# Dilated attention in a decoder layer: the small matmuls of a block gathered into two groups

## The chip, the cores and the metric

The kernel runs on one core of one Trainium2 chip. The metric is the device time of one execution in microseconds (us). The engines are TensorE (PE in the profile, with its weight loads as PEld), VectorE (DVE), ScalarE (ACT), GpSimd (POOL) and SyncE (SP), which issues the DMAs. Each runs its own instructions in the order in which the program gives them, and waits for others through semaphores.

## What is computed

One decoder layer for 1024 tokens of width 1024, in float32: an attention with three groups of dilated windows, then a gated MLP with a short convolution. The change lies in the attention. Cut to that, the reference is:

```python
h = rms_norm(x, mixer_norm)
proj = (h @ w_in).reshape(B, S, 3, 3, 8, 64)          # group, q/k/v, head, width
for g, (window, dilation) in enumerate(((128, 1), (512, 4), (2048, 16))):
    q = rms_norm(proj[:, :, g, 0], q_gain[g]) * 64 ** -0.5
    k = rms_norm(proj[:, :, g, 1], k_gain[g])
    # blocks of 128 queries of one residue class see themselves and the block before
    s = where(mask, q @ k.T, -inf)
    lse = logsumexp(s);  o = exp(s - lse) @ v
weights = softmax(stack(lses))                        # over the three groups
x = x + sum(weights * outs) @ w_out
x = x + (silu(gate) * up) @ w_down                    # MLP, left as it is
```

## The kernel before

**Units and blocks.** The attention is cut into six units: group 2, 1, 0, each in two halves of four heads (`units`, units 0 to 5). A unit has eight blocks of 128 tokens, so there are 48 blocks, numbered 0 to 47. A block in the first place of its residue class sees only itself (`nk` = 1: all blocks of units 0 and 1, every second one of units 2 and 3, and the first of units 4 and 5); the others see the block before too (`has_prev`, `nk` = 2).

**Large and small matmuls of a block.** `project(k)`, k = 0 to 7, makes q and k of the block in the PSUM tile `qk`: three matmuls of 512 columns for each k (lines 207 to 209), because every operand is kept as a rounded high part and a low part. `project_v(k)` does the same for v in the tile `vp` with three of 256 columns (lines 216 to 218). These two are the main stream of TensorE. The tile `qk` has two PSUM buffers and `vp` has one (`bufs=1`).

Between them stand the small matmuls: `heads_T` (tile `tr`, four transposes of q and k), `scores` (tile `s`, 6 matmuls for nk = 1, or 12 on half the rows for nk = 2), `weights_T` twice (tile `pt`, 2 or 4 transposes of the softmax weights each time), `attend` twice (tile `u`, 4 or 8 matmuls each). Below, tr4, s6, pt2, u8 and so on mean so many matmuls of that tile in a row.

**Work on the other engines.** For each block, in this order: `norm` (ACT squares `qk`, line 223; DVE sums it, line 225; POOL takes the root), `values` (ACT copies `vp` to `v`, line 236; DVE subtracts to get the low part, line 237; after that `vp` is free for the next block), `scale` (DVE, line 229), `heads_split` (ACT and DVE empty `tr` into qT and kT), `softmax` (four times a DVE operation on `s` and an exponential on ACT, lines 320 and 323), `weights_split` twice (ACT and DVE empty `pt` into `pT`, lines 337 and 338), `finish` (DVE reduces `u`, line 356; in units 4 and 5 `merge` follows with one more DVE operation, line 398).

**What sets the order.** Every step is put into a list with a time (`at(...)`), the list is sorted by time, and each engine gets its instructions in that order. One unit of that time is one k of `project`, and a block takes eight. For block i the steps start from e = 8 i + 8, and the table `T` holds each step's offset, so `w0=8.3` puts the first `weights_T` at e + 8.3. A `project_v(k)` stands at 8 i + 0.85 k + 2.6. The offset `bd` is added to `scores` and `softmax` of blocks without a block before. These times only order the instructions; on the chip each starts when its operands and buffers are ready.

**PSUM.** Eight banks: `qk` 2, `vp` 1, `u` 1, tag `tr` 2 (for `tr` and `pt`), tag `s` 2 (for the two halves of the scores; in unit 0 also `xT`, the transposes of the normed input).

**After the attention.** From N = 384 on that time axis, `out_project` (tile `y`) with its weight tiles `wo` takes the place of the main stream, while the last two blocks of attention are still being finished.

Of the kernel before, what the change touches and what calls it, by code (L numbers as in the profile page):

```python
# [8 lines left out]
F32 = mybir.dt.float32  # L9
# [8 lines left out]
P = 128  # L18
# [13 lines left out]
LA = 2  # L32


T = dict(v=2.6, vs=0.85, w=3.1, norm=-0.2, val=0.6, kept=3.2, scale=2.5, hT=4.2, hs=4.45, sc=6.45,
         sm=6.5, w0=8.3, ws0=9.35, w1=10.0, ws1=11.95, mw=10.0, a0=12.2, a1=13.3, mo=12.2,
         fin=14.4, t0=4, so0=3.2, so1=3.3, so2=5.1, so3=5.2, to0=-3.43, to=-3.6, n2=3.0, n2s=5.8,
         xf=-9.8, xs=-5.0, xt=-3.5, wp=1, bd=0.5, bh=0)


@with_exitstack
def trunk(ctx: ExitStack, tc: tile.TileContext, x, mixer_norm, ffn_norm, w_in, q_gain, k_gain,
# [47 lines left out]
    pa = tc.tile_pool(name="pa", bufs=1, side="right", reuse_waits="tile")  # L90
# [4 lines left out]
    PA = ppa.__enter__()  # L95
# [96 lines left out]
    class Block:  # L192
# [67 lines left out]
                        nc.gpsimd.tensor_copy(kT[hd, z, :, :P], self.prev.own(z, e))  # L260

        def heads_T(self):
            self.tr = PA.tile([P, 4, P], F32, name="tr", tag="tr", bufs=2)
            for j in range(4):
                nc.tensor.transpose(self.tr[:, j], self.qn[:, 2 * j:2 * j + 2], ident)  # L265

# [58 lines left out]

        def weights_T(self, p):
            lo, nk = self.lo, self.nk
            self.pt[p] = pt = PA.tile([P, 2, nk, P], F32, name="pt", tag="tr", bufs=2)
            for e in range(2):
                for j in range(nk):  # L330
                    nc.tensor.transpose(pt[:, e, j], self.sm[:, 2 * p + e, lo + j * P:lo + (j + 1) * P],
                                        ident)
# [74 lines left out]
    def at(t, f, *args):  # L407
        plan.append((t, len(plan), f, args))

    xs = {}  # L410
# [48 lines left out]
    for i in range(8):  # L459
        t = early[i] if i < 2 else (8 * i - 12, 8 * i + T["xf"], 8 * i + T["xs"], 8 * i + T["xt"])  # L460
        at(t[0], get_x, i)
# [19 lines left out]
    for u in range(6):  # L481
        wt = {}
        for kt in range(KT):
# [3 lines left out]
            elif kt < SP:  # L487
                t = 64 * u - 32 + T["wp"] + 4 * kt
                lead = t - 3
            else:  # L490
                t = 64 * u - KT + (3.9, *((8.7, 9.45, 10.6, 12.6) if u % 2 == 0 else (5.4, 8.7, 9.6, 10.8)))[kt - SP]
                lead = max(t - 8, 64 * u - KT + (kt - SP - 3) * 1. + T["w"] + .5) if kt < SP + 3 else wt[kt - 3] + .3
            wt[kt] = t
            at(lead, load_raw, u, kt)
            at(t, load_w, u, kt)
    for i, b in enumerate(blocks):
        b.prev = blocks[i - 1] if b.has_prev else None
        for k in range(KT):
            at(8 * i + k, b.project, k)
            at(8 * i + T["vs"] * k + T["v"], b.project_v, k)  # L500
        e = 8 * i + 8
        for name, (step, *args) in dict(
                norm=(b.norm,), val=(b.values,), kept=(b.kept,), scale=(b.scale,), hT=(b.heads_T,),
                hs=(b.heads_split,), sc=(b.scores,), sm=(b.softmax,), w0=(b.weights_T, 0),
                ws0=(b.weights_split, 0), w1=(b.weights_T, 1), ws1=(b.weights_split, 1),
                mw=(b.merge_weights,), a0=(b.attend, 0), a1=(b.attend, 1), mo=(b.merge_others,),
                fin=(b.finish,)).items():
            late = not b.has_prev and (T["bd"] if name in ("sc", "sm") else T["bh"] if name in ("hT", "hs") else 0)
            if b is blocks[-1] and name in ("norm", "val"):
                late = 1.5 if name == "norm" else .3  # L510
            at(e + T[name] + late, step, *args)


    N = 8 * len(blocks)
# [6 lines left out]
    class M:  # L521

        wo, ol, oT, x1, n2, h, pt = {}, {}, {}, {}, {}, {}, {}
# [301 lines left out]
            at(t + 14.6 + .5 * (i == 5), odd, i, 1, nc.gpsimd)  # L825
            at(t + 14.7 + .5 * (i == 5), odd, i, 2, nc.vector)
    t = N + T["t0"] + 42
    at(N + 15, lambda: pa.__exit__(None, None, None))
    at(N + 15.1, make_bt)
    at(t - 20, conv_consts, 0)  # L830
    at(t - 12, conv_consts, 1)
    at(t - 12, pairs[0].load)
# [164 lines left out]
    for n in range(3, NF + 1):  # L997
        old, p, new = pairs[n - 1], *((pairs + [None] * 3)[n:n + 2])
# [7 lines left out]
        if p is None:  # L1006
            for m in range(8):
                b, i = divmod(m, 4)
                pool, tag, bufs = (M.PL, "b", 2) if m < 2 else (M.PR, "ac"[m % 2], 3)
# [97 lines left out]
```

## Time and profile before

| | |
|---|---|
| median of 3 runs | 1303.2 us (1301.95 to 1303.62) |
| the profiled execution: its time, its span | 1301.99 us, 1300.0 us |
| TensorE busy, of the span | 1274.2 us (98%) |
| VectorE, ScalarE, GpSimd busy | 896.2, 617.1, 486.7 us |
| attention without its start and end, 25 to 578 us | TensorE busy 548.79 of 553.00 us |
| end of the attention, 578 to 612 us | TensorE busy 30.55 of 34.00 us |
| the rest, to the end | TensorE busy 678.90 of 688.00 us |

The time is that of the whole execution; the span is from the first instruction to the last in the profile. TensorE's matmuls overlap, and the ends that the profile gives them are modelled, so the starts of successive matmuls tell more than their durations: in the main stream a matmul of 512 columns starts some 0.23 us after the one before, and one of 256 columns some 0.12 us. "Idle before" in a row counts only gaps over 0.15 us.

### The profile page before, as it was taken

The page shows a single profiled execution, that of the slowest core. Times are in us where ns is not written, and L with a number is a line of the kernel's source. Part 1 is how long each engine was busy: PE and PEld are TensorE (multiplying, and loading weights), DVE is VectorE, ACT ScalarE, POOL GpSimd, SP SyncE. Part 2 cuts the span into 40 slices and gives each one's busy share as a digit, 9 for nine tenths or more (in the row PEclk, how much of TensorE's full clock was granted, in tenths as well). Part 3 has the DMA queues.
Part 4 walks back from the last instruction along what each step waited for, and adds up shares of the span by engine and source line. Part 5 has one row for each costly group of instructions (what it writes and reads, how often), then busy time and mean ns, then how long its engine had stood idle before and what let it go on. Part 6 is the DMA issues. An engine that isn't in the chain of part 4 may idle for free.

```text
span 1300.0 us, 19219 instructions
## 1 busy us (share of the span) xinstructions
PE 1274.2 (98%) x6911; PEld 1071.0 (82%) x6911; DVE 896.2 (69%) x1542; ACT 617.1 (47%) x1284; POOL 486.7 (37%) x596
## 2 busy tenths in 40 slices
PE   7999999999999999999998999999999999999998
PEld 6888888888888888887886788888888887888887
DVE  5665555555555665557876988888888888876664
ACT  5555454444464454345644454544544545444441
POOL 4333443332454555535523544444444442000000
PEclk9999999999999999999999999999999999999999
DMA  7112112111131221023711333233233229963341
GB/s 263 38 54 79 38 38 60 47 48 52 46 109 51 62 63 37 27 70 132 235 35 43 120 122 122 81 114 105 66 122 122 81 81 326 367 212 97 97 143 63
DMA packets 111614, 132.16 MB, mean 102 GB/s; under 512 B 6126, under 2 KB 80030, under 8 KB 111518
## 3 DMA queue, kind: packets, MB, share of 16 engines
q1 hardware_dynamic: 111518, 130.93, 31.5%
q8 instruction: 55, 0.90, 0.3%
q14 instruction: 41, 0.34, 0.1%
HBM read 95.91 MB, written 35.00 MB: 101 GB/s over the span
## 4 chain that ended last, share of the span: by engine, by line
PE 43%; DVE 4%; ACT 2%; issue 1%; DMA 1%; POOL 0%; SPq 0%; DVEq 0%; POOLq 0%; ACTq 0%
PE y L902 15%; PE ua L718 15%; PE uc L718 8%; PE ub L718 4%; DVE c L763 2%; ACT c L761 1%; DMA x<-in_x 1%; DMA graw<-gde 0%; DVE bt L629 0%; DVE sz L691 0%; DVE c L774 0%; DVE xn L595 0%; DMA wB<-in_ffn_w_down 0%; DVE sy L687 0%; POOL b L629 0%
## 5 line engine op out<-in xcount | busy, mean ns | idle before, releaser
L902 PE MATMUL y<-wd,g 128*128 128x512 f32 x924 | 210.4, 389 | 0.2
L902 PEld LDWEIGHTS y<-wd,g 128*128 128x128 f32 x924 | 173.4, 188 | 36.9 <-DVE wd L629 0.6
L207 PE MATMUL qk<-w,hh 128*128 128x512 f32 x384 | 157.5, 410 | 0.1
L208 PE MATMUL qk<-w,hh 128*128 128x512 f32 x384 | 152.8, 398 | 0.3 <-DVE w L189 0.3
L209 PE MATMUL qk<-w,hl 128*128 128x512 f32 x320 | 126.1, 394 | 0.0
L79 POOL TENSOR_SCALAR ms<-ss 128x8 f32<-128x8 f32 (+1 forms) x64 | 12.8, 201 | 296.6 <-DVE ss L225 254.0
L763 DVE SCALAR_TENSOR_TENSOR c<-uu,cw,c 128x1023 f32<-128x1023 f32 (+1 forms) x44 | 97.0, 2205 | 37.1 <-ACT c L761 36.3
L216 PE MATMUL vp<-w,hh 128*128 128x256 f32 x384 | 122.0, 318 | 0.4 <-DVE v L237 0.2
L217 PE MATMUL vp<-w,hh 128*128 128x256 f32 x384 | 107.9, 281 | 0.0
L549 POOL TENSOR_TENSOR wyl<-sy,wyh 128x1024 fp32r<-128x1024 f32 x21 | 56.9, 2708 | 109.3 <-issue 55.3
L80 POOL TENSOR_TENSOR rs<-ms,half 128x8 f32<-128x8 f32 (+1 forms) x64 | 89.0, 1391 | 5.3
L218 PE MATMUL vp<-w,hl 128*128 128x256 f32 x320 | 90.0, 281 | 0.0
L323 ACT ACTIVATE sm<-sm,ust 128x128 f32<-128x128 f32 (+1 forms) x128 | 53.3, 418 | 77.0 <-DVE ust L320 74.5
L216 PEld LDWEIGHTS vp<-w,hh 128*128 128x128 f32 x384 | 72.8, 189 | 15.2 <-DVE v L237 2.4
L225 DVE TENSOR_REDUCE ss<-qn 128x8 f32<-128x512 f32 x48 | 32.9, 685 | 75.6 <-ACT qn L223 75.6
L276 ACT ACTIVATE qT<-tr,gains 128x256 fp32r<-128x256 f32 x48 | 22.7, 474 | 122.0 <-PE tr L265 122.0
L217 PEld LDWEIGHTS vp<-w,hh 128*128 128x128 f32 x384 | 72.8, 190 | 9.1
L279 DVE SCALAR_TENSOR_TENSOR qT<-tr,gains,qT 128x256 fp32r<-128x256 f32 x48 | 23.1, 482 | 81.4 <-ACT kT L278 81.4
L208 PEld LDWEIGHTS qk<-w,hh 128*128 128x128 f32 x384 | 73.1, 190 | 1.5 <-DVE w L189 1.0
L207 PEld LDWEIGHTS qk<-w,hh 128*128 128x128 f32 x384 | 73.0, 190 | 0.7 <-ACT hh L116 0.5
L320 DVE CUSTOM_DVE_ANT_0 sm<-s,mask 128x128 f32<-128x128 f32 (+1 forms) x192 | 56.0, 347 | 24.0 <-PE s L298 18.5
L209 PEld LDWEIGHTS qk<-w,hl 128*128 128x128 f32 x320 | 60.5, 189 | 14.6 <-DVE hl L117 0.2
(193 smaller groups left out, 3395.7 us busy)
## 6 DMA issues: line engine op xcount, KB each, us to landing
uraw<-in_ffn_w_up SPq DMA_DIRECT2D x44, 512.0 KB
raw<-in_attn_w_in SPq DMA_DIRECT2D x48, 384.0 KB
wB<-in_ffn_w_down SPq DMA_DIRECT2D x44, 256.0 KB
graw<-gds SPq DMA_DIRECT2D x44, 256.0 KB
gdo<-c SPq DMA_DIRECT2D x11, 512.0 KB
gds<-gbc SPq DMA_DIRECT2D x11, 512.0 KB
graw<-gdo SPq DMA_DIRECT2D x22, 256.0 KB
ud<-ust SPq DMA_DIRECT2D x32, 132.0 KB
```

What stands on the lines that cost most here:

```text
L80: nc.gpsimd.tensor_tensor(r[:, :n], t[:, :n], half[:, :n], op=ALU.pow)
L207: nc.tensor.matmul(self.qk, a, w[:, 0, :512], start=k == 0, stop=False)
L208: nc.tensor.matmul(self.qk, a, w[:, 1, :512], start=False, stop=False)
L209: nc.tensor.matmul(self.qk, b, w[:, 0, :512], start=False, stop=k == KT - 1)
L216: nc.tensor.matmul(self.vp, a, w[:, 0, 512:], start=k == 0, stop=False)
L217: nc.tensor.matmul(self.vp, a, w[:, 1, 512:], start=False, stop=False)
L218: nc.tensor.matmul(self.vp, b, w[:, 0, 512:], start=False, stop=k == KT - 1)
L320: nc.vector.tensor_tensor_reduce(out=sm[:, h, lo:], in0=src[h], in1=m, op0=ALU.add, op1=ALU.min, scale=-1.0, scalar=3e38, accum_out=st[:, ...
L549: eng.tensor_sub(l, raw, h.bitcast(F32))
L718: nc.tensor.matmul(acc[:, lo:hi], w[z][:, s + k], a[y][:, j, k, lo:hi], start=begin and lo == 0 and k == 0 and n == 0, stop=k == 3 and n == 2,
L763: nc.vector.scalar_tensor_tensor(c[:, k:], u[:, :S - k], cw[:, 2 - k, j:j + 1], c[:, k:], op0=ALU.mult, op1=ALU.add)
L902: nc.tensor.matmul(y, gs[:, z, ts], ws[:, w], start=f and n == 0, stop=k == NK - 1 and n == 2, skip_group_check=True)
```

## The change

In each block the small matmuls now stand in two groups. The first has both `weights_T` of a block and `heads_T` of the next block; the second has `scores` of that next block and both `attend` of the block. To that end the table `T` is changed, and PSUM is shared out otherwise: `heads_T` takes a buffer of the tag `s` in all units but the first, and for nk = 1 the two `weights_T` write two halves of one tile. Closing the pool of the attention's tiles moves from N + 15 to N + 17.2, since `finish` is later.

```diff
-T = dict(v=2.6, vs=0.85, w=3.1, norm=-0.2, val=0.6, kept=3.2, scale=2.5, hT=4.2, hs=4.45, sc=6.45,
-         sm=6.5, w0=8.3, ws0=9.35, w1=10.0, ws1=11.95, mw=10.0, a0=12.2, a1=13.3, mo=12.2,
-         fin=14.4, ...
-         xf=-9.8, xs=-5.0, xt=-3.5, wp=1, bd=0.5, bh=0)
+T = dict(v=2.6, vs=0.85, w=3.1, norm=-0.2, val=0.6, kept=3.2, scale=2.5, hT=4.2, hs=4.45, sc=7.01,
+         sm=7.06, w0=12.1, ws0=12.5, w1=12.15, ws1=12.55, mw=10.0, a0=15.02, a1=15.03, mo=12.2,
+         fin=16.1, ...
+         xf=-9.8, xs=-5.0, xt=-3.5, wp=1, bd=0, bh=0)
...
-            self.tr = PA.tile([P, 4, P], F32, name="tr", tag="tr", bufs=2)
+            self.tr = PA.tile([P, 4, P], F32, name="tr", tag="s" if self.u else "tr", bufs=2)
...
-            self.pt[p] = pt = PA.tile([P, 2, nk, P], F32, name="pt", tag="tr", bufs=2)
+            if nk == 2:
+                self.pt[p] = PA.tile([P, 2, nk, P], F32, name="pt", tag="tr", bufs=2)
+            else:
+                if p == 0:
+                    self.pt4 = PA.tile([P, 4, 1, P], F32, name="pt", tag="tr", bufs=2)
+                self.pt[p] = self.pt4[:, 2 * p:2 * p + 2]
+            pt = self.pt[p]
...
-    at(N + 15, lambda: pa.__exit__(None, None, None))
-    at(N + 15.1, make_bt)
+    at(N + 17.2, lambda: pa.__exit__(None, None, None))
+    at(N + 17.3, make_bt)
```

TensorE, a block without a block before, before the change: the row ahead of the scores, the scores (tile `s`, two halves), and what follows up to the first transposes of the weights.

```order
L218 MATMUL vp<-w,hl 128x256
L294 MATMUL s_1865<-kT,qT 128x256 x3
L294 MATMUL s_1866<-kT,qT 128x256 x3
L207 MATMUL qk<-w,hh 128x512
L208 MATMUL qk<-w,hh 128x512
L209 MATMUL qk<-w,hl 128x512
L216 MATMUL vp<-w,hh 128x256
L217 MATMUL vp<-w,hh 128x256
L218 MATMUL vp<-w,hl 128x256
L207 MATMUL qk<-w,hh 128x512
L208 MATMUL qk<-w,hh 128x512
L209 MATMUL qk<-w,hl 128x512
```

The same place with the change, from the last `project` of the block to the first `project_v` behind the group.

```order
L209 MATMUL qk<-w,hl 128x512
L295 MATMUL s_1846<-kT,qT 128x256 x3
L295 MATMUL s_1847<-kT,qT 128x256 x3
L356 MATMUL u<-v,pT 128x128
L358 MATMUL u<-v,pT 128x64
L356 MATMUL u<-v,pT 128x128
L358 MATMUL u<-v,pT 128x64
L356 MATMUL u<-v,pT 128x128
L358 MATMUL u<-v,pT 128x64
L356 MATMUL u<-v,pT 128x128
L358 MATMUL u<-v,pT 128x64
L216 MATMUL vp<-w,hh 128x256
```

The scores stood ahead of the last `project` of the next block and now stand behind it, with both `attend` right behind them. From the scores to the first `project_v` (k = 0) of the block after, TensorE had s6 qk vp qk pt2 vp qk pt2 qk; it now has s6 u8 vp qk vp qk qk. For nk = 2 it had s12 vp qk vp qk pt4 vp qk pt4 qk, and now has s12, u8 or u16 (by the block whose weights are attended), vp qk vp qk qk.

VectorE, unit 5, before the change, from the sum of squares of a block on (`ss`: `norm`; `v`: `values`; `mt<-u` and `o`: `finish` and `merge`):

```order
L225 TENSOR_REDUCE ss_6795<-qn 128x8
L237 TENSOR_TENSOR v<-vp,v 128x4x64
L338 TENSOR_TENSOR pT<-pt,pT 128x512
L370 TENSOR_REDUCE nm<-mt 128x4
L372 TENSOR_TENSOR e<-nm,mt 128x12
L229 TENSOR_TENSOR qn<-qk,rs 128x512
L338 TENSOR_TENSOR pT<-pt,pT 128x512
L386 RECIPROCAL rz<-z 128x4
L279 SCALAR_TENSOR_TENSOR qT<-tr,gains,qT 128x256
L282 SCALAR_TENSOR_TENSOR kT<-tr,gains,kT 128x2x128
L356 TENSOR_REDUCE mt<-u 128x256
L398 TENSOR_TENSOR o<-mt,f 128x256
```

VectorE at the same place with the change (line 363 is the old line 356, 405 the old 398):

```order
L225 TENSOR_REDUCE ss_6764<-qn 128x8
L363 TENSOR_REDUCE mt<-u 128x256
L405 TENSOR_TENSOR o<-mt,f 128x256
L237 TENSOR_TENSOR v<-vp,v 128x4x64
L377 TENSOR_REDUCE nm<-mt 128x4
L379 TENSOR_TENSOR e<-nm,mt 128x12
L229 TENSOR_TENSOR qn<-qk,rs 128x512
L393 RECIPROCAL rz<-z 128x4
L280 SCALAR_TENSOR_TENSOR qT<-tr,gains,qT 128x256
L283 SCALAR_TENSOR_TENSOR kT<-tr,gains,kT 128x2x128
```

The reduction of `u`, and in units 4 and 5 the merge behind it, stood ahead of the softmax and now stand between the sum of squares and the low part of `v`; both subtractions of `pT` have moved behind qT and kT.

## Rows read from the trace of the kernel before

**Rows 1.** The page's first line.

```profile
span 1300.0 us, 19219 instructions
```

**Rows 2.** Stretches: us, PE, PEld, DVE, ACT, POOL busy (count), clock, DMA.

```profile
25.00:578.00 553.00, 548.79 (x3670) 482.67 (x3671) 318.72 (x887) 268.54 (x778) 240.06 (x447) 1.00 0.18 54
578.00:612.00 34.00, 30.55 (x182) 24.33 (x179) 23.82 (x53) 18.69 (x45) 17.18 (x27) 1.00 0.39 134
```

**Rows 3.** TensorE's waits, 25 to 578: who waited for whom, us, times, longest.

```profile
PE tr L265 <- DVE qn L229: 2.9, 5, 0.9
PE pt L331 <- ACT sm L323: 0.3, 1, 0.3
...
PE vp L216 <- DVE v L237: 0.2, 1, 0.2
```

**Rows 4.** Timeline of TensorE, unit 4: start, duration, engine, line, tile, count.

```profile
408.19 0.38 PE L331 MATMUL pt<-ident,sm 128*128 128x128 f32 x2
408.33 0.48 PE L207 MATMUL qk<-w,hh 128*128 128x512 f32 x1
408.64 0.39 PE L208 MATMUL qk<-w,hh 128*128 128x512 f32 x1
...
409.11 0.28 PE L216 MATMUL vp<-w,hh 128*128 128x256 f32 x1
...
409.45 0.40 PE L207 MATMUL qk<-w,hh 128*128 128x512 f32 x1
...
410.16 0.27 PE L216 MATMUL vp<-w,hh 128*128 128x256 f32 x1
...
413.46 0.22 PE L349 MATMUL u<-v,pT 128*128 128x128 f32 x1
...
413.82 0.36 PE L216 MATMUL vp<-w,hh 128*128 128x256 f32 x1
414.02 0.28 PE L217 MATMUL vp<-w,hh 128*128 128x256 f32 x1
```

**Rows 5.** Timeline of DVE there, block 33, behind scores of nk = 1.

```profile
407.66 0.69 DVE L225 TENSOR_REDUCE ss<-qn 128x8 f32<-128x512 f32 x1 [1.71 <-ACT qn L223]
408.26 0.41 DVE L237 TENSOR_TENSOR v<-vp,v 128x256 fp32r<-128x256 f32 x1
```

**Rows 6.** Timeline of DVE and PE, block 34, behind scores of nk = 2.

```profile
419.73 0.41 DVE L237 TENSOR_TENSOR v<-vp,v 128x256 fp32r<-128x256 f32 x1
...
420.79 0.28 PE L216 MATMUL vp<-w,hh 128*128 128x256 f32 x1
```

**Rows 7.** Timeline of DVE: `finish` and `merge` of a block in unit 4.

```profile
414.02 0.69 DVE L356 TENSOR_REDUCE mt<-u 128x256 f32<-128x512 f32 x1
414.82 0.46 DVE L398 TENSOR_TENSOR o<-mt,f 128x256 f32<-128x256 f32 x1
```

**Rows 8.** Timeline of DVE and PE where `vp` was late, block 7.

```profile
105.69 0.42 DVE L237 TENSOR_TENSOR v<-vp,v 128x256 fp32r<-128x256 f32 x1
...
106.16 0.38 PE L216 MATMUL vp<-w,hh 128*128 128x256 f32 x1
106.38 0.28 PE L217 MATMUL vp<-w,hh 128*128 128x256 f32 x1
```

**Rows 9.** Timeline of PE and DVE in unit 0, with `xT`.

```profile
63.07 1.04 PE L114 MATMUL xT<-ident,xn 128*128 128x128 f32 x8
...
65.66 1.29 DVE L117 TENSOR_TENSOR hl<-xT,hh 128x512 fp32r<-128x512 f32 x2
...
66.85 0.87 PE L294 MATMUL s<-kT,qT 128*128 128x256 f32 x6
```

More of the change, by code (lines that the diff above doesn't have):

```diff
@@ L32 @@
 LA = 2
-T = dict(v=2.6, vs=0.85, w=3.1, norm=-0.2, val=0.6, kept=3.2, scale=2.5, hT=4.2, hs=4.45, sc=6.45,
-         sm=6.5, w0=8.3, ws0=9.35, w1=10.0, ws1=11.95, mw=10.0, a0=12.2, a1=13.3, mo=12.2,
-         fin=14.4, t0=4, so0=3.2, so1=3.3, so2=5.1, so3=5.2, to0=-3.43, to=-3.6, n2=3.0, n2s=5.8,
-         xf=-9.8, xs=-5.0, xt=-3.5, wp=1, bd=0.5, bh=0)
+T = dict(v=2.6, vs=0.85, w=3.1, norm=-0.2, val=0.6, kept=3.2, scale=2.5, hT=4.2, hs=4.45, sc=7.01,
+         sm=7.06, w0=12.1, ws0=12.5, w1=12.15, ws1=12.55, mw=10.0, a0=15.02, a1=15.03, mo=12.2,
+         fin=16.1, t0=4, so0=3.2, so1=3.3, so2=5.1, so3=5.2, to0=-3.43, to=-3.6, n2=3.0, n2s=5.8,
+         xf=-9.8, xs=-5.0, xt=-3.5, wp=1, bd=0, bh=0)
 @with_exitstack
```

## Prediction

> **What bounds the kernel now.** [...] Then the waits: the transposes of the heads wait for VectorE's scaling of q and k, 2.9 us in five places; everything else over 0.15 us is small, with one wait of `vp` for VectorE's low part of `v` (0.2 us) [rows 3]. That last row matters most here, because `vp` has one buffer: the first `project_v` of a block cannot start before VectorE has done line 237 of the block before. In most blocks this wait is absent, but the room is small. Behind scores of nk = 1, VectorE ends `v` at 408.26 + 0.41 = 408.67 [rows 5] and TensorE starts `vp` at 409.11 [rows 4]: a slack of 0.44 us. Behind scores of nk = 2 it is 420.79 - 420.14 = 0.65 us [rows 6]. The work of the change is to move things on both sides of this slack, so I follow it through.
>
> **What a small matmul costs.** Two transposes start at 408.19, and the main stream goes on at 408.33; its next matmul follows 0.31 us later instead of 0.23 (408.33 to 408.64) [rows 4]. So the two cost 0.14 + 0.08 = 0.22 us, 0.11 each. Four matmuls of `attend` cost 413.82 - 413.46 = 0.36, and 0.08 for the late second matmul behind them (413.82 to 414.02, against 0.12), together 0.44 us, 0.11 each [rows 4]. A group costs its number of matmuls times 0.11 us, whether it has two or four, and I find no fixed price for a group. The change neither adds nor removes a matmul, so gathering them gives TensorE nothing by itself: I take 0, with a bound that the rival below prices. One step of `project_v` takes 409.45 - 409.11 = 0.34 us and one of `project` 410.16 - 409.45 = 0.71 us [rows 4].
>
> **The slack of `vp`, step by step.** The chain on the other side is: scores, four exponentials of the softmax, the square of `qk`, the sum of squares, (now also `finish`), the low part of `v`. It starts with the scores, so I count from there. The order of TensorE between the scores and the next `vp` loses one `project` (0.71), and both `weights_T`, and gains both `attend`; with nk = 2 it loses one `project_v` (0.34) besides. VectorE's chain gains the reduction of `u`. A reduction of the same 0.69 us lets the next operation start 0.60 us later (407.66 to 408.26) [rows 5], so I take 0.60. In units 4 and 5 it also gains the merge: the start moves from 414.02 to 414.82, and then 0.46 less the overlap of 0.09 [rows 5, 7], so 0.80 + 0.37 = 1.17 in all.
>
> Scores of 6, attend of 8 (16 blocks of units 0 to 2): 0.44 - 0.71 - 0.44 + 0.88 - 0.60 = -0.43 us.
> Scores of 12, attend of 8 (8 blocks): 0.65 - 0.34 - 0.71 - 0.88 + 0.88 - 0.60 = -1.00 us.
> Scores of 12, attend of 16, with the merge (10 blocks of units 4 and 5): 0.65 - 0.34 - 0.71 - 0.88 + 1.76 - 1.17 = -0.69 us.
> Scores of 12, attend of 8, with the merge (2 blocks): -1.00 - 0.57 = -1.57 us.
> Scores of 6, attend of 16: 0.44 - 0.71 - 0.44 + 1.76 - 0.60 = +0.45 us, no wait (8 blocks); with the merge -0.12 (1 block).
>
> A negative slack is a wait of TensorE, and a wait costs a little more than its lateness. Block 7 shows it: `v` ends at 106.11, `vp` starts at 106.16, and its second matmul comes 0.22 us later (106.38) instead of 0.12, since its weights were not loaded ahead [rows 8]. So 0.05 + 0.10 = 0.15 us are added each time. That gives 16 x 0.58 = 9.3, 8 x 1.15 = 9.2, 10 x 0.84 = 8.4, 2 x 1.72 = 3.4 and 0.3: **30.6 us of new waits**. Nothing covers them, since all that is queued behind the waiting `vp` on TensorE is the main stream, and the chain starts anew from each block's scores, so a wait in one block doesn't buy slack in the next.
>
> **Other new waits.** In unit 0, `xT` and the scores share two buffers. VectorE ends the second low part of `xT` at 65.66 + 1.29 = 66.95, and the scores need that buffer for their second half at 66.85 + 3 x 0.12 = 67.21 [rows 9]: a slack of 0.26. With the change both subtractions of `pT` stand ahead of that low part. They are as long as line 237 (0.41, less the overlap of 0.09, so about 0.32 each [rows 5]); TensorE comes 0.71 - 0.44 = 0.27 later. Slack 0.26 - 0.64 + 0.27 = -0.11, so 0.26 us in each of six blocks: 1.6 us. In the other units `tr` and `s` share the tag `s`, but the scores wait for the emptying of `tr` anyway, as qT and kT. The transposes of the weights and the `attend` now come microseconds after their softmax and their split, and should wait for nothing.
>
> **What goes.** TensorE reaches `heads_T` later in its row than VectorE reaches `scale`, which also lost a subtraction of `pT` ahead of it. So I let the five waits of `tr` go: 2.9 + 5 x 0.10 = 3.4 us (bounds 0 and, with every idle time of the stretch, 4.2 [rows 2, 3]). At the end of the attention, 34.00 - 30.55 = 3.45 us are idle [rows 2], in part because scores, softmax, weights and `attend` of the last blocks follow each other closely with no main stream between. They now stand further apart. I take 2.0 us (bounds 0 and 3.45), since the split of the output weights, which TensorE also waits for there, is not moved. That `finish` of the last block is later costs nothing as far as I see: the tiles that reuse its memory are written after two more `out_project`, some 12 x 0.23 us each.
>
> **The sum.** 30.6 + 1.6 - 3.4 - 2.0 = +26.8 us on the profiled execution's 1302.0 us: 1328.8 us. That execution is 1.2 us below the median of the runs, within their spread.
>
> **Rivals.**
> *Only the blocks with 12 scores wait.* If the start of `finish` or of the square overlaps more than I count, the 16 blocks at -0.43 lose most of their wait, and the others some 0.4 us each. The sum is then 8 x 0.75 + 10 x 0.44 + 2 x 1.3 = 13 us, less 5.4: 1310 us. For it speaks that -0.43 is a difference of five numbers; against it, that the durations repeat from block to block.
> *Faster: the chain to `v` is never last.* Should VectorE's `v` be ready in time in all blocks (it would have to come 0.58 us earlier in most and 1.15 us in eight), only what goes is left: 1302.0 - 5.4 = 1296.6 us. The order of VectorE, with the reduction of `u` ahead of `v`, speaks against it.
> *A group has a fixed price.* If the 0.08 us by which the main stream is late behind a group were paid once per group and not for the last weight load, 239 groups becoming 98 would give 141 x 0.08 = 11.3 us. With the waits of `vp` that is 1317.5 us; without them, 1285. Against it: 0.22 for two and 0.44 for four leave no room for a constant [rows 4]. [...]
> [...]
>
> **How the numbers follow.** Chances: the forecast 0.80, with its own range from 1316 (the wait costs its lateness alone, the 16 blocks wait 0.3 us, the end gives 3.45) to 1338 (the waits of `tr` stay, the end gives nothing, and blocks at the change of units, with weight splits on VectorE, wait a microsecond more); only blocks with 12 scores 0.09; never last 0.06; fixed price 0.03; clock 0.02. The range from 1308 to 1338 holds the first two. Within 0.2% (2.6 us, about what a measurement of this kernel can tell from no change) lies only a mixture of these, 0.03. Faster has 0.07, slower 0.90.
>
> **What would show it.** Right: a wait of `vp` line 216 for DVE line 237 at the top of TensorE's waits, some 36 times, 0.4 to 1.6 us each, longest where 12 scores stand before 8 of `attend`; no wait in the blocks with 6 scores and 16 of `attend`; the row of `tr` gone; VectorE's timeline with the reduction of `u` between line 225 and line 237. Wrong: `vp` starting 0.2 us or more after VectorE's `v` has ended, a granted clock under 1.00 in the attention, or matmuls of a group spaced closer than 0.11 us.

## The result and the profile after

The changed kernel takes 1342.5 us (median of four runs, 1341.6 to 1343.0) against 1302.6 for the kernel before: 1.031 times as long, with a 95% interval from 1.0295 to 1.032. The profiled execution has a span of 1340.9 us, 40.9 more than [rows 1]. The direction of the forecast (1329, slower) was right, its size was not: 40 us were lost where 26.8 were counted, and the time lies above the range.

All of the loss lies before the MLP. In the timelines of TensorE the last `qk` starts at 616.36 instead of 579.34 (+37.0), the last `y` of the output projection at 687.54 instead of 646.67 (+40.9), and the end comes 40.9 later too. The first line of the page after, and the first rows of TensorE's waits (who waited for whom, us in total, times, longest; line 237 is still the low part of `v`, 266 is `heads_T`, 188 and 189 are the high and low part of the weights, 117 the low part of `xT`):

```profile
span 1340.9 us, 19130 instructions
```

```profile
PE vp L216 <- DVE v L237: 25.2, 34, 2.7
...
PE s L295 <- DVE hl L117: 3.5, 5, 0.7
PE qk L207 <- ACT w L188: 2.2, 2, 1.7
...
PE tr L266 <- DVE qn L229: 1.3, 2, 0.9
...
PE qk L208 <- DVE w L189: 1.0, 2, 0.5
```

The row of `vp` was one wait of 0.2 us in [rows 3]; it is now the first of all. The row of `tr` fell from five waits to two, of which one stands in the attention and one behind it. New are `s` behind `xT`, and `qk` behind weights. The stretch of the attention (columns as in [rows 2]) shows that TensorE is still the engine with the most work, but idle for 31.7 of 575 us instead of 4.2 of 553, and that the clock was not quite full:

```profile
25.00:600.00 575.00, 543.28 (x3544) 471.12 (x3543) 308.04 (x861) 261.43 (x760) 230.72 (x433) 0.99 0.16 50
```

A regular block of unit 4 (scores of 12, `attend` of 16, with the merge), DVE and then PE (start, duration, engine, line, operation, tile):

```profile
461.04 0.69 DVE L225 TENSOR_REDUCE ss<-qn 128x8 f32<-128x512 f32 x1 [1.66 <-ACT qn L223]
461.64 0.68 DVE L363 TENSOR_REDUCE mt<-u 128x256 f32<-128x512 f32 x1
462.43 0.42 DVE L405 TENSOR_TENSOR o<-mt,f 128x256 f32<-128x256 f32 x1
462.77 0.42 DVE L237 TENSOR_TENSOR v<-vp,v 128x256 fp32r<-128x256 f32 x1
...
463.24 0.39 PE L216 MATMUL vp<-w,hh 128*128 128x256 f32 x1 [0.59 <-DVE v L237]
463.46 0.28 PE L217 MATMUL vp<-w,hh 128*128 128x256 f32 x1
```

In [rows 5] line 237 followed line 225 directly. Now `finish` and the merge stand between, 1.13 us from start to start (461.64 to 462.77). `v` ends at 463.19, `vp` starts 0.05 later, and its second matmul comes 0.22 later instead of 0.12: the wait costs what [rows 8] said. The weight loads of these two matmuls (PEld), first at [rows 8] in the kernel before, then here, and for comparison in the kernel before where `vp` doesn't wait [rows 4]:

```profile
106.16 0.19 PEld L216 LDWEIGHTS vp<-w,hh 128*128 128x128 f32 x1 [0.58 <-DVE v L237]
106.27 0.19 PEld L217 LDWEIGHTS vp<-w,hh 128*128 128x128 f32 x1
```

```profile
463.24 0.19 PEld L216 LDWEIGHTS vp<-w,hh 128*128 128x128 f32 x1 [1.02 <-DVE v L237]
463.35 0.19 PEld L217 LDWEIGHTS vp<-w,hh 128*128 128x128 f32 x1
```

```profile
408.88 0.19 PEld L216 LDWEIGHTS vp<-w,hh 128*128 128x128 f32 x1
409.11 0.19 PEld L217 LDWEIGHTS vp<-w,hh 128*128 128x128 f32 x1
```

Without a wait the first load starts 0.23 us ahead of its matmul and the second with the first matmul (409.11); behind the wait the first starts with its matmul (463.24) and the second 0.11 later, 0.11 ahead of its own.

**Where the 40.9 us are.** To add waits up I take, for each pair of neighbouring TensorE instructions, the time from start to start over the usual one of the same kind. The table has all such delays over 0.14 us, by what released them (us, attention alone unless said). The late second matmul behind a wait of `vp` is 0.10 and has a row of its own. The end is taken from the first `qk` of the last block to the last `y`, so that it holds the same matmuls before and after; the wait of `vp` in it (0.8) stands in the rows above and is taken out here.

| | before | after | change | counted in the prediction |
|---|---|---|---|---|
| `vp` for `v`, its first matmul | 0.9 | 30.6 (34 waits) | +29.7 | +30.6, with the next row |
| the late second matmul behind it | 0.3 | 3.6 | +3.3 | in the row above |
| scores for `xT`'s low part, unit 0 | 0 | 4.3 (5) | +4.3 | +1.6 |
| `qk` for weights, at unit boundaries | 0.6 | 4.1 (4) | +3.4 | 0 |
| `tr` for `qn` | 3.8 | 0.6 (1) | -3.2 | -3.4 |
| `pt` for the softmax | 0.7 | 0 | -0.7 | 0 |
| the end, first `qk` of the last block to last `y` | 79.3 | 80.3 | +1.0 | -2.0 |
| two stretches at half clock | 0 | about 3.4 | +3.4 | 0 |
| sum | | | +41.2 | +26.8 |

The sum is 0.3 more than the 40.9 measured; the rest lies at the start and in differences below 0.14. So the large term was 2.4 us short, and four others were missing, too small or had the wrong sign. The rest of this text is about both.

### The profile page after: what moved, and what is told of

Its sections match the earlier page's. It is cut to its first block, busy times and chain, and to the rows that moved or that the text cites. A ratio compares the mean times of both kernels' runs of the same rounds, so it can differ in the third digit from the quotient of the medians.

```text
span 1340.9 us, 19130 instructions
## 1 busy us (share of the span) xinstructions
PE 1286.7 (96%) x6911; PEld 1073.9 (80%) x6911; DVE 895.4 (67%) x1542; ACT 616.7 (46%) x1284; POOL 484.0 (36%) x596
## 3 DMA queue, kind: packets, MB, share of 16 engines
q1 hardware_dynamic: 111518, 130.93, 30.6%
## 4 chain that ended last, share of the span: by engine, by line
PE 43%; DVE 4%; ACT 1%; issue 1%; POOL 1%; DMA 0%; SPq 0%; DVEq 0%; POOLq 0%; ACTq 0%
PE ua L725 16%; PE y L909 15%; PE uc L725 8%; PE ub L725 4%; DVE c L770 1%; ACT c L768 0%; DVE bt L636 0%; DMA wB<-in_ffn_w_down 0%; DVE xn L602 0%; POOL b L636 0%; DVE sz L698 0%; DVE x L595 0%; POOL wzl L556 0%; POOL wxl L556 0%; DVE c L781 0%
## 5 line engine op out<-in xcount | busy, mean ns | idle before, releaser
L216 PE MATMUL vp<-w,hh 128*128 128x256 f32 x384 | 119.4, 311 | 25.2 <-DVE v L237 25.2
```

What stands on the lines that cost most here:

```text
L216: nc.tensor.matmul(self.vp, a, w[:, 0, 512:], start=k == 0, stop=False)
```

## Experiments

Each is a change to one of the kernels; the numbers are medians, with the kernel before (1302.1 to 1302.8) run beside them on the same chip.

**1. Finish behind `v`.** One number of the table:

```diff
-         fin=16.1,
+         fin=16.7,
```

> The changed kernel, with one number of the table other: fin 16.7 instead of 16.1, so that a block's finish (and merge) stands behind the next values on VectorE and no longer ahead of them. Chain theory (scores, softmax, Square, its sum, finish, v, then vp): each wait of vp falls by the 0.60 us of the finish, by 1.17 where merge goes with it. From the waits of the changed kernel: 16 blocks 0.41 to 0, 8 blocks 1.05 to 0.45, 10 blocks 0.73 to 0, 2 blocks 1.60 to 0.43, the four long ones at unit boundaries by 0.6 each: -6.6 -4.8 -7.3 -2.3 -2.4 = -23, so about 1319 us, vp's waits about 4 us in sum instead of 25.2. Rival: what holds v is the copy of vp on ScalarE or the exponentials, not the finish: no change, 1342. Second rival: the finish now delays the scale of the heads, and waits of tr take the place of half of the gain: 1330.

Measured: 1326.5 us, 15.9 less than the changed kernel (1.0182 of before, 1.0167 to 1.0197).

```profile
PE vp L216 <- DVE v L237: 8.0, 15, 2.2
...
PE tr L266 <- DVE qn L229: 2.7, 4, 0.9
```

So `finish` ahead of `v` is on the path. From start to start the waits of `vp` fell from 30.6 to 10.4, and the late second matmuls behind them from 3.6 to 1.6, together by 22.2 us. Against this, 1.7 came back as waits of `tr` (the second rival, but far smaller than it said), 0.6 as waits of `qk` for low parts, the second stretch at half clock was twice as long (about 1.7; the mean granted clock of the profiled run is 0.995, in the changed kernel 0.997), and the end, taken as in the table, is 1.2 longer, with more waits for output weights. The four longest waits fell by 0.5 to 0.6 each, about as expected. What was too large in the 23 is its first term: of the 16 waits of 0.41 the changed kernel has eight.

**2. Scores apart again.** Scores and softmax go back ahead of the last projection; all else stays:

```diff
-sc=7.01,
-         sm=7.06,
+sc=6.45,
+         sm=6.5,
...
-bd=0,
+bd=0.5,
```

> The changed kernel with scores and softmax back ahead of the last projection (sc 6.45, sm 6.5, bd 0.5), so that scores and attend no longer stand together; the transposes of weights and heads stay one group, attend and finish stay late. Chain theory: scores end a projection of 0.69 us earlier (0.69 and a step of vp, 1.02, in blocks with a previous one), and the waits of vp fall by that: 0.41 to 0, 1.05 to 0.03, 0.73 to 0, 1.60 to 0.58: -6.6 -8.2 -7.3 -2.0, the four long ones -2.8, and the clock's two falls behind waits go, -3: -30, so about 1312. Rival, that a group has a price of its own: 48 more groups at 0.08 to 0.1 give 4 to 5 us back, 1317. Rival, that the waits come from the finish's place alone: the finish stays where it is, 1342.

Measured: 1326.4 us (1.0182, 1.0166 to 1.0197), half of what was expected.

```profile
PE vp L216 <- DVE v L237: 6.5, 6, 2.4
PE s L295 <- DVE hl L117: 6.3, 5, 1.3
```

In units 2 to 5 most regular blocks wait no more for `vp`, as the chain says (in unit 5 a block takes 12.60 us instead of 13.43): there a projection more between scores and `vp` is enough. Of the six waits that the row has left, four stand where the changed kernel had its longest ones. But the scores, 0.7 us earlier, wait longer for `xT` in unit 0, and come too early for the split of the heads elsewhere: in a block of unit 1 the six scores take 0.93 us to the next instruction's start instead of 0.71, `vp` is still 0.22 late instead of 0.42, and the block takes 11.4 us as without this edit. The clock, too, is still at half for 6.8 us in all, where I had expected no fall. So the place where the change put the scores has a reason of its own, and 1312 was out of reach by this edit.

**3. Room for a second `vp`.** The wait's cause is taken away: `vp` shares three buffers with the weights' transposes, in the order of instructions of the changed kernel.

```diff
-                self.vp = PA.tile([P, 256], F32, name="vp", bufs=1)
+                self.vp = PA.tile([P, 512], F32, name="vp", tag="tr", bufs=3)[:, :256]
...
-        tag, bufs = ("vp", 1) if i else ("s", 2)
+        tag, bufs = ("tr", 3) if i else ("s", 2)
```

> The changed kernel in its order of instructions, but vp shares three buffers with the weights' transposes instead of having one of its own, so that a block's first product of values need not wait for the copy of the block before. Chain theory: all waits of vp go (25.2 us), and with the two long ones the falls of the clock (3 to 4 us); nothing else is late in a block, since the next user of the chain is attend, seven projections later: about 1314 us. Rival, that the wait only moves to the next that needs VectorE (tr, whose scale stands behind v, or s, behind the softmax): half of it comes back, 1328. Waits of s in unit 0 (3.5 us), of qk at the boundaries and the tail stay in either case.

Measured: 1314.4 us (1.0093, 1.0078 to 1.0109), the number of the chain theory.

```profile
PE qk L207 <- ACT w L188: 4.1, 4, 1.8
PE tr L266 <- DVE qn L229: 3.3, 5, 1.0
PE s L295 <- DVE hl L117: 3.0, 5, 0.7
PE qk L208 <- DVE w L189: 2.0, 4, 0.5
```

No wait of `vp` is left; 28.1 us of the 40 are gone, and one of the two stretches at half clock with them (the mean granted clock is 0.999 instead of 0.997). But the number was met by luck. From start to start 34.2 us of `vp` and about 1.7 of the clock went, and 6.4 came back: `qk` is now late for weights by 7.8 us instead of 4.1, and `tr` by 3.3 instead of 0.6. So the waits did move in part, as the rival said, by a fifth instead of half; the expectation missed this, and missed as much on the other side, since it took the 25.2 us of idle time in the row of `vp` and not the delay from start to start (30.6) with the second matmuls (3.6).

The run also settles whether gathering pays: the distance from one block's first `qk` to the next one's, in undisturbed blocks, is 10.89 us in unit 1 and 12.60 in unit 5 with this order, 10.85 and 12.57 in the kernel before. Two groups in a block instead of five save nothing.

**4. The buffers alone.** The kernel before in its own order, with the change's two edits of buffers: `tr` under the tag `s` (unit 0 apart), and one tile `pt4` for both halves of a block's turned weights.

```diff
-            self.tr = PA.tile([P, 4, P], F32, name="tr", tag="tr", bufs=2)
+            self.tr = PA.tile([P, 4, P], F32, name="tr", tag="s" if self.u else "tr", bufs=2)
...
+                if p == 0:
+                    self.pt4 = PA.tile([P, 4, 1, P], F32, name="pt", tag="tr", bufs=2)
+                self.pt[p] = self.pt4[:, 2 * p:2 * p + 2]
```

> The kernel before in its own order, with the change's buffers alone: heads' transposes in the scores' buffers, both weight transposes of a block without a previous one in one tile. If the order alone costs, this is as fast as before or gains what the five waits of tr hold, 2.9 us: 1299.7 to 1302.6. If the buffers cost too (the scores wait for the heads' copies, or the second transposes for the first copy out of the shared tile), waits of s or pt appear and it is slower, by 0.2 to 0.4 in each of 40 blocks: 1310 to 1318.

Measured: 1347.5 us (1.034, 1.0323 to 1.0357), more than the changed kernel itself.

```profile
PE pt L337 <- DVE pT L344: 34.0, 26, 3.4
```

The second half of the weights is turned only after the first half has been copied out, since both lie in one tile; I had allowed 0.4 us for it, and it is up to 3.4. In the changed kernel both halves are turned before either is copied, so this price isn't paid there. It shows that buffers and order of this change belong together. What `tr` under the tag `s` costs alone was not tried. But where a block before exists, so that each half of the weights has its own tile, a block of units 4 and 5 takes 12.57 us here as in the kernel before, so `tr` under `s` costs nothing there.

**5. Three stretches, one at a time.** On the kernel of experiment 3. First unit 0, where the copies of the turned weights stood ahead of `xT`'s second low part:

```diff
+            late += .3 if not b.u and name in ("ws0", "ws1") else 0
             at(e + T[name] + late, step, *args)
```

> The kernel with shared buffers for vp (1314.4 us), and in the first unit the copies of the turned weights stand behind the second low part of xT on VectorE and ScalarE, no longer ahead of it. Theory, that the scores' second half waits there because two copies of weights stand ahead of the low part: the five waits of s for hl go, 3.8 us from start to start, and nothing else in unit 0 is near: about 1310.6. Rival, that the low part is late for its own chain (transposes, copy, subtraction): they stay, 1314. Second rival: the copies of weights that now come later make attend wait for pT: 1312 to 1314, with waits of u.

Measured: 1312.6 us. The five waits of `s` are gone, so the theory of the place holds; but of 3.8 us a wait of `tr` in unit 0 (0.85) and later starts of `xT` and `tr` there (0.28 and 0.12 us in block 4, each too short to be a row of the waits) took back half.

Then the boundaries:

```diff
-(2.62, 3.47, 4.6, 5.3, 6.1, 7.3, 8.65)
+(2.62, 3.47, 4.6, 5.3, 8.61, 8.63, 8.65)
...
-(8.7, 9.45, 10.6, 12.6)
+(6.9, 8.62, 10.6, 12.4)
```

> The kernel with shared buffers for vp (1314.4 us), with its copies at the two boundaries where tokens are put in another order moved: the reordering copy that stood ahead of the softmax's exponentials behind the values, the weights' fifth load ahead of the softmax, the sixth ahead of the last reordering copy, the eighth ahead of the copies of the turned weights. Theory, that qk waits there for weights whose casts stand in ScalarE's queue behind the late softmax: the waits of qk (4.8 for the cast and 2.7 for the low part from start to start) go, and with the wait of 1.9 us goes the fall of the clock at 204 us (some 1.5 us): about 1306. Rival, that ScalarE itself has too much to do there: the waits move to the scores or tr, 1311 to 1314.

Measured: 1313.5 us, the rival. All waits of `qk` for weights went, and `tr` waits 2.97 and 2.73 us at the same two places, because a weight's low part now stood on VectorE ahead of the softmax. The clock fell behind both (the mean of the run is 0.997, in experiment 3 it was 0.999).

Then the end, with the old places for the last two blocks:

```diff
+OLD = dict(sc=6.45, sm=6.5, w0=8.3, ws0=9.35, w1=10.0, ws1=11.95, a0=12.2, a1=13.3, fin=14.4)
...
-            at(e + T[name] + late, step, *args)
+            off = OLD.get(name, T[name]) if i > 45 else T[name]
+            at(e + off + late, step, *args)
```

> The kernel with shared buffers for vp (1314.4 us), whose last two blocks keep the places of the kernel before (scores ahead of the last projection, weights in two groups, attend and finish early). Theory, that the end of the attention loses 3.9 us because the last blocks' late steps find no projection beside them (last qk to first y 5.6 us against 3.3 before, first to last y 65.6 against 64.1): both go back, about 1310.5. Rival, that the end is long for the output weights' casts alone: unchanged, 1314.

Measured: 1313.5 us, 0.8 less, which is no more than the runs beside it differ. In the trace the end goes back altogether: from the first `qk` of the last block to the last `y` it is 79.3 us instead of 80.3, as in the kernel before (79.3). So 1.0 us is the order's doing, and the 3.9 of the expectation compared unlike work. From the last `qk` to the first `y`, for instance, it is 4.96 here, 5.62 in the kernel of experiment 3 and 3.27 before; the 1.69 between 4.96 and 3.27 are 16 matmuls of `attend` (16 x 0.11 = 1.8) that now stand behind the last `qk`.

All three together:

> All three edits on the kernel with shared buffers for vp. If each is its own stretch, the gains add: 1314.4 - 3.8 - 8.5 - 3.9 = about 1298, which would be 0.3% under the kernel before: the groups then cost nothing and save the waits of tr. If a group has a price of its own (0.08 us for each), there would be 48 fewer in this kernel than in the one before and it would come to some 4 us less still, 1294. If the waits move rather than go: 1305 to 1310.

Measured: 1310.0 us (1.0061, 1.0046 to 1.0076). TensorE, its timeline at the first of the two boundaries:

```profile
199.58 0.60 PE L339 MATMUL pt<-ident,sm 128*128 128x128 f32 x4
203.14 1.09 PE L267 MATMUL tr<-ident,qn 128*128 128x128 f32 x4 [2.96 <-DVE qn L230]
```

**6. The boundaries once more.** Two of VectorE's instructions ahead of the softmax go to GpSimd, and the low part of the next weight behind `scale`:

```diff
-nc.scalar.copy if k % 2 else nc.vector.tensor_copy)
+nc.scalar.copy if k % 2 else nc.gpsimd.tensor_copy if k == 4 else nc.vector.tensor_copy)
...
+            if u in (2, 4) and kt == 5:
+                at(64 * u - KT + 10.55, low_w, u, kt)
```

> The kernel with all three edits (1310.0 us), where tr waited 3.13 and 2.90 us at the two boundaries because VectorE did a reordering copy (0.9) and a weight's low part (0.95) ahead of the softmax. Now GpSimd, idle there for 4.7 us, does both; the low part of the next weight stands behind the scale of the heads; in the odd units one weight's load goes behind the scale too (tr waited 1.16 at 112). Theory, that VectorE's queue ahead of the softmax makes the wait: the two waits go (6.0 us), the two falls of the clock behind them (3.4 us each at half speed, so some 1.5 each) and the 1.2: 1310.0 - 6.0 - 3.0 - 1.2 = 1299.8, just under the kernel before. Rival, that GpSimd is too slow for them: waits of qk for its low parts, 1305 to 1310.

Measured: 1308.8 us (1.0054, 1.0041 to 1.0066). At unit 4 the wait is gone (that block takes 12.30 us instead of 15.67); at unit 2 it stayed (2.76; that block takes 16.41 us instead of 15.42), since GpSimd now had a copy (1.17 us) and a low part (1.86) more to do ahead of the `rs` that `scale` needs, which starts at 201.37 instead of 199.80. Mostly the rival.

**7. The price of a group.** The same with scores and softmax apart, as in experiment 2:

> The same with scores and softmax apart from attend again (sc 6.45, sm 6.5, bd 0.5). Neither order waits for vp with shared buffers, so this prices a group alone, read from the lengths of undisturbed blocks (10.89 in unit 1, 12.60 in unit 5 of the kernel with scores beside attend) and from the whole. Theory, that a group has no price: the same blocks within 0.05 and the same time within 2 us, 1298 to 1302. Rival, 0.08 for each group more: 10.97 and 12.68, and 48 of them make 3.8 us, 1303.6.

Measured: 1313.0 us (1.0085, 1.0071 to 1.0099; its profiled run 1310.9, its runs up to 1316.2). By the whole, 4.2 us more than in experiment 6, the theory missed (it had 2 at most) and the rival's 3.8 would fit; the blocks decide against it. In unit 5 a block takes 12.60 us with either order, so no price of 0.08 for a group. In unit 1 it takes 11.10 instead of 10.89, and the difference is inside the scores, as in experiment 2. TensorE's timeline of six scores in unit 1, first of this kernel, then of the one of experiment 6:

```profile
149.66 1.10 PE L302 MATMUL s<-kT,qT 128*128 128x256 f32 x6
```

```profile
150.31 0.87 PE L302 MATMUL s<-kT,qT 128*128 128x256 f32 x6
```

**8. The waits of `tr` without regrouping.** The change did remove them, so I tried on the kernel before what the traces name as their cause: a weight's low part ahead of `scale` on VectorE.

```diff
+            if u and kt == 5:
+                at(64 * u - KT + 10.55, low_w, u, kt)
```

> The kernel before, with one thing moved: from the second unit on, the low part of the weights' sixth block (one subtraction of 0.95 us on VectorE) stands behind the scale of the heads instead of ahead of it. Theory, that the five waits of tr (2.9 us, 3.8 from start to start) are VectorE's queue at the units' starts and need no regrouping of the matmuls: they go, 1302.5 - 3.8 = about 1298.7, 0.3% faster than before. Rival, that the projection then waits for the low part: qk waits of 0.3 to 0.8 in the five units, 1300 to 1303.

Measured: 1302.3 us against 1302.2 (1.0000, 0.9991 to 1.0009). All five waits of `tr` are gone, and the rival took their place:

```profile
PE qk L213 <- DVE w L195: 2.5, 4, 1.3
```

No kernel here beats the one before.

## Why the prediction was right, and where not

**What bounds the kernel: right.** One buffer for `vp`, and a chain from the scores to VectorE's low part of `v`. Experiment 3 takes away the buffer's limit and gets 28.1 us back; experiments 1 and 2 shorten the chain at either end, and the regular blocks' waits shrink or go.

**The price of a small matmul: right.** Nothing is saved by gathering. The blocks of experiment 3 are 0.03 us longer than those of before, with the same number of matmuls. In the four matmuls of `attend` in [rows 4] and the two of `vp` behind them the weight loads start 0.11 to 0.12 us apart, as long as a small matmul is counted; the first and the last of them:

```profile
413.34 0.19 PEld L349 LDWEIGHTS u<-v,pT 128*128 128x128 f32 x1
413.46 0.19 PEld L351 LDWEIGHTS u<-v,pT 128*128 128x128 f32 x1
413.57 0.19 PEld L349 LDWEIGHTS u<-v,pT 128*128 128x128 f32 x1
...
413.79 0.19 PEld L216 LDWEIGHTS vp<-w,hh 128*128 128x128 f32 x1
413.90 0.19 PEld L217 LDWEIGHTS vp<-w,hh 128*128 128x128 f32 x1
```

The rival of a fixed price is out.

**The new waits of `vp`: right by kind, 3.6 us short in sum (34.2 against 30.6; 1.2 of this stood in the kernel before).** By kind, with the late second matmul: scores 12 and attend 8: 1.16 (counted 1.15); with the merge 1.71 (1.72); scores 12, attend 16 and merge 0.84 (0.84). These three add up to 21.1 us where 21.0 were counted, so slack, `finish` and merge were read rightly. Scores 6 and attend 8 wait 0.52 where regular (0.58). What the sum lacks are four long waits, 1.92, 1.26, 2.94 and 1.26, where 0.58 was counted three times and at the last none: three at changes of units, one where VectorE makes the masks just ahead of a softmax. I had put "a microsecond more" there into the range, not into the sum. In part this is made up for by unit 0, where the scores wait already and only two blocks have a wait of `vp`.

**Step that failed, the boundaries.** ScalarE and VectorE, timelines at the start of unit 2 (line 144 puts tokens in another order, 188 casts weights, 324 is an exponential, 223 the square, 363 `finish`):

```profile
203.17 1.14 ACT L144 CAST hh<-hh 128x512 fp32r<-128x512 f32 x2 [0.88 <-DVE hh L144]
204.22 0.40 ACT L324 ACTIVATE sm<-sm,ust 128x128 f32<-128x128 f32 x1
...
205.78 0.57 ACT L223 ACTIVATE qn<-qk 128x512 f32<-128x512 f32 x1
...
207.54 1.57 ACT L188 CAST w<-raw 128x768 fp32r<-128x768 f32 x2
```

```profile
203.00 0.28 DVE L321 CUSTOM_DVE_ANT_0 sm<-s,mask 128x128 f32<-128x128 f32 x1
...
206.38 0.69 DVE L225 TENSOR_REDUCE ss<-qn 128x8 f32<-128x512 f32 x1 [1.27 <-ACT qn L223]
206.99 0.68 DVE L363 TENSOR_REDUCE ust<-u 128x256 f32<-128x512 f32 x1
207.58 0.41 DVE L237 TENSOR_TENSOR v<-vp,v 128x256 fp32r<-128x256 f32 x1
```

The softmax's first row was ready at 203.3, but the first exponential starts at 204.22, behind two reordering copies. Square, sum, `finish` and `v` follow late, `vp` waits 2.65 us, and the weights' casts queue behind all of it, so `qk` waits for a cast and then for its low part (1.73 and 0.50 us at 217). I followed the chain through regular blocks only and did not ask what else ScalarE carries at the two places where a unit changes its order of tokens. At the three changes of units above, the waits of `vp` are 5.0 us more than counted, and those of `qk` for weights, for which the prediction had nothing, 3.4.

**Step that failed, the clock.** The sum has no term for it, and a fall had a chance of 0.02. The groups of 8 and 12 transposes run at 1.00 (from 25 to 208 us and from 222 to 600; one of 12, 465.4 to 467.0, at 1.00). The clock fell behind waits, which no step had. TensorE behind the wait of 2.65 us, and the stretch (its clock is the figure 0.55):

```profile
208.05 0.44 PE L216 MATMUL vp<-w,hh 128*128 128x256 f32 x1 [2.65 <-DVE v L237]
...
208.72 0.63 PE L207 MATMUL qk<-w,hh 128*128 128x512 f32 x1
209.14 0.63 PE L208 MATMUL qk<-w,hh 128*128 128x512 f32 x1
```

```profile
207.90:211.60 3.70, 3.55 (x12) 3.07 (x13) 2.52 (x4) 1.94 (x3) 2.85 (x2) 0.55 0.35 107
```

The projections' matmuls start 0.42 apart instead of 0.23; from 208.3 to 211.6 the clock is 0.50. A second such stretch (0.50 from 218.5 to 221.8) follows the waits of 1.73 and 0.50 at 217. So the wait of 2.65 us cost about 1.7 more than itself (3.70 us at 0.55). The prediction's own sign for "wrong", a clock under 1.00 in the attention, was met.

**Step that failed, unit 0.** Slack 0.26 - 0.64 + 0.27 was to give a wait of 0.1; it is 0.74. DVE and PE:

```profile
67.42 0.69 DVE L117 TENSOR_TENSOR hl<-xT,hh 128x512 fp32r<-128x512 f32 x1
68.02 0.41 DVE L345 TENSOR_TENSOR pT<-pt,pT 128x256 fp32r<-128x256 f32 x1
68.88 0.42 DVE L345 TENSOR_TENSOR pT<-pt,pT 128x256 fp32r<-128x256 f32 x1 [0.44 <-ACT pT L344]
69.36 0.69 DVE L117 TENSOR_TENSOR hl<-xT,hh 128x512 fp32r<-128x512 f32 x1
...
70.11 0.62 PE L295 MATMUL s<-kT,qT 128*128 128x256 f32 x3 [0.74 <-DVE hl L117]
```

In [rows 9] the two low parts of `xT` followed each other. Now two subtractions of `pT` stand between, and I counted 0.64 for them as if they ran back to back. But the second waits 0.44 for ScalarE, whose copy of the second half starts at 68.47, 0.04 after VectorE's first subtraction has ended: from 68.02 to 69.36 they take 1.34. The term was the right one, short by 0.70. Experiment 5 in unit 0 (the edit of `ws0`) confirms the place.

**Step that failed, the end.** "They now stand further apart" was to give 2.0 us back; 1.0 was lost. PE and ACT there (line 635 casts output weights, 582 copies the turned heads' output):

```profile
616.67 0.98 PE L299 MATMUL s<-kT,qT 64*128 64x256 f32 x12
617.58 0.33 PE L356 MATMUL u<-v,pT 128*128 128x128 f32 x1
...
620.19 0.60 PE L580 MATMUL otr<-ident,ol 128*128 128x128 f32 x4
621.98 0.50 PE L591 MATMUL y<-wo,oT 128*128 128x512 f32 x1 [1.20 <-ACT wo L635]
```

```profile
619.70 0.49 ACT L324 ACTIVATE sm<-sm,mt 128x256 f32<-128x256 f32 x1
620.83 0.59 ACT L582 CAST oT<-otr 128x512 fp32r<-128x512 f32 x1 [0.54 <-PE otr L580]
621.31 1.14 ACT L635 CAST wo<-wraw 128x512 fp32r<-128x512 f32 x2
```

From the last `qk` to the last `y` it is 71.2 us instead of 67.3, but 12 matmuls of the scores and 16 of `attend` have moved behind that `qk` (28 x 0.11 = 3.1, the first rows); over the same work, from the first `qk` of the last block on, the loss is 1.0. Two waits went, as I had counted (`pt` for the softmax 0.9, `u` for `pT` 0.4). In their place TensorE waits for output weights 3.2 us instead of 1.9, and 0.9 for `tr`. The last softmax is later, so the output weights' casts behind it on ScalarE are later too, and TensorE has no projection left to put under them. I had said that the split of the output weights "is not moved"; its place in the order isn't, but what stands ahead of it is. Experiment 5 gives the 1.0 back by the old places.

**What goes: right.** The waits of `tr` fell about as counted (-3.2 against -3.4). Whether they are worth having is another matter: experiment 8 removes them without any regrouping and wins nothing, since the low part that was moved is then what TensorE waits for.

## What to carry to other kernels

Gathering small matmuls has no value of its own where each is paid by itself (0.11 us each here); what counts is which chain through the other engines a move lengthens, and how much of TensorE's work is left to cover it. Follow that chain not only in the regular block but at each place where the engines on it carry extra work (a change of units, the first unit with its inputs, the end), since here the same move cost two to five times as much there, and the longest wait, 2.65 us, cost the clock as well (0.50 behind it). A term read from back-to-back durations is too small where two engines take turns: count from start to start over the whole pair. And when a change moves work over the edge of a stretch, compare stretches that hold the same work: the end seemed to lose 3.9 us here and lost 1.0.

## What the runs showed of the hardware

**The clock fell behind some short waits and not behind others.** In the kernel of experiment 3 it fell behind waits of `qk` of 1.76 and 0.49 us: the projections' matmuls behind them start up to 0.46 us apart instead of 0.23 (204.09, 204.55). In the kernel of the end's edit (experiment 5) the same two waits stood at the same place, and the stretch behind them has a clock of 1.00:

```profile
203.39 0.50 PE L208 MATMUL qk<-w,hh 128*128 128x512 f32 x1 [1.76 <-ACT w L189]
204.38 0.51 PE L209 MATMUL qk<-w,hh 128*128 128x512 f32 x1 [0.49 <-DVE w L190]
```

```profile
203.00:212.00 9.00, 5.61 (x30) 4.16 (x30) 5.56 (x9) 4.68 (x9) 4.09 (x6) 1.00 0.48 146
```

In the kernel of experiment 4, with waits of up to 3.38 us, there were seven stretches at half clock (0.50 from 216.9 to 223.7 in one; the mean of the run is 0.989). In that of experiment 1, with a mean of 0.995, the clock fell in the MLP too, behind a wait of 1.28 us at 728; the changed kernel has the same wait there (1.30 at 744.93) and no fall (1.00 from 730 to 760). What decides in the cases between is not settled by these runs.

**VectorE's subtraction took longer beside one of GpSimd's.** The same subtraction of a weight's low part took 0.96 us on VectorE alone and 2.61 us when GpSimd began one of its own 0.02 us earlier. DVE and POOL, in the kernel of experiment 8:

```profile
196.09 0.96 DVE L195 TENSOR_TENSOR w<-raw,w 128x768 fp32r<-128x768 f32 x1 [1.01 <-ACT w L188]
...
197.90 2.61 DVE L195 TENSOR_TENSOR w<-raw,w 128x768 fp32r<-128x768 f32 x1
```

```profile
197.88 1.83 POOL L195 TENSOR_TENSOR w<-raw,w 128x768 fp32r<-128x768 f32 x1 [1.12 <-ACT w L188]
```

The longest wait of experiment 8, 1.28 us of `qk`, is this. 2.61 stands against 0.96 of VectorE's alone and 1.83 of GpSimd's, 2.79 together. It shows elsewhere, too: in the kernel of all three edits (experiment 5) the subtraction takes 1.96 us where GpSimd began 0.69 earlier, and in the kernel of experiment 6 two of them in a row take 3.07 where it began 0.43 earlier. In the kernel before, the 30 on VectorE have a median of 0.96 us and a longest of 2.24, and GpSimd's 18 a median of 1.83 and a longest of 2.53. In experiment 6 I moved a low part to GpSimd, and in experiment 8 one beside GpSimd's, without counting this.
